# The values of stick-breaking attention: two blocks of tokens side by side in each unit of weights

## The chip, the cores and the metric

The kernel runs on one core of one Trainium2 chip. The metric is the device time of one execution in microseconds, the median of several runs. The core's engines work from instruction queues of their own and meet by semaphores: TensorE (PE in the profile; PEld is its loading of stationary operands), VectorE (DVE), ScalarE (ACT), GpSimd (POOL) and SyncE (SP), which here issues most of the transfers.

## What is computed

A decoder trunk of two layers on 512 tokens of 1024 features: a convolution layer, then an attention layer, each between two half-step SwiGLU networks. The residual stream behind the first layer is normed once and projected to keys and values that the attention layer shares. What the change touches is the attention with its projections:

```python
kv = rms_norm(h, kv_norm) @ w_kv              # 1024 -> 2 x 1024
k_flat, v_flat = jnp.split(kv, 2, axis=-1)
k_shared, v_shared = split_heads(k_flat), split_heads(v_flat)   # 16 heads of 64
...
q = split_heads(u @ attn_w_q[i])
z = einsum('bhqd,bhkd->bhqk', qb, kb) * scale
log_one_minus = where(causal, log_sigmoid(-z), 0)
log_remain = cumsum(log_one_minus, reverse) - log_one_minus
weights = where(causal, exp(log_sigmoid(z) + log_remain), 0)
out = einsum('bhqk,bhkd->bhqd', weights, vb)
```

All is in fp32, and the result must be that of fp32 products.

## The kernel before

Each fp32 operand is split into a high and a low part (`split`: a cast on ACT at L247, a subtraction on DVE at L248), and a product is three matmuls, high by high, high by low and low by high, one after the other into the same PSUM bank (`mm3`, L392 to L395; the trace shows them by these lines). Weights come as units of 128 rows by 1024 columns. `fetch` loads one on SP into `raw`, ACT casts it into `whi`, DVE makes `wlo`; each of the three has 3 buffers. `unit` hands out the next one that was begun and begins another.

Attention runs on 16 heads, two to a pair p. `project_values(i)` makes the values of four heads, i from 0 to 3: 256 columns for 512 tokens, from two units of weights, each of which holds four of the eight input chunks of 128 features. Its tokens go in four blocks b of 128. For a block, a chunk of the split input (`kvh`, `kvl`, 128 features by 128 tokens) is the stationary operand and 256 columns of the weights move; 8 chunks by 3 matmuls make 24 matmuls into one bank `pv`. Then for each of two pairs of heads, q = 0 and 1, ACT copies 128 columns into the tile `vs` (L1129, the high part) and DVE subtracts that from the bank (L1130, the low part). `project_keys(p)` makes the keys and queries of a pair of heads in banks `pk` and `pq`, each with 24 matmuls of 512 columns. `head(p, e)` is one head: scores into `z` (4 banks), a cumulative sum as matmuls of `sh` and `sl` with triangular constants into `z` (L1188), weights `w` split into `wh` and `wl` on DVE or GpSimd (L1232, L1233), products with `vs` into `av` (2 banks, L1239 and L1241), and at the end `low` on ACT (L1245) and a matmul that swaps halves (L1246). The names carry numbers: `z8_1` belongs to head 8, `pv1_0` to the values unit 1, block 0; `vs2` and `vs3` hold the values of unit 1, `vs6` and `vs7` those of unit 3.

PSUM has 8 banks; in attention 4 are of kind z, 2 of kind av, and 2 of kind pj. The banks of kind pj serve `pv`, `pk` and `pq` in turn, and at the end `po`, the output projection. Which projection is written behind which head stands in a table: unit 0 of the values and pair 0 ahead of all heads, units 1 to 3 behind heads 3, 7 and 11.

```python
PROJECTIONS = (
    (("v", 0), ("kq", 0)), (("kq", 1), ("kq", 2)), (("v", 1),), (("kq", 3), ("kq", 4)), (("v", 2),),
    (("kq", 5), ("kq", 6)), (("v", 3),), (("kq", 7),),
)
```

The order on the engines is not the written one. A scheduler places every instruction of the attention by a simulated timeline, and the matmuls of the projections fill the places in which a head waits for the other engines. So a new order in `project_values` gives new places to instructions of the heads too. The instructions on each engine run in the order that the scheduler fixed, each behind its semaphores.

Of the kernel before, what the change touches and what calls it, by code (L numbers as in the profile page):

```python
# [6 lines left out]
F32 = mybir.dt.float32  # L7
# [7 lines left out]
P = 128  # L15
D = 1024
T = 512
NC = D // P
# [67 lines left out]
PJ_BANKS = 2  # L86
# [110 lines left out]
def decoder_kernel(ctx, tc, xin, gu, dna, dnb, pw1, pw2, kq, wv, wo, out):  # L197
    nc = tc.nc
    V, A, G, PE = nc.vector, nc.scalar, nc.gpsimd, nc.tensor

    def pool(c, name, bufs=1, space=None):
        kw = {"space": space} if space is not None else {}
        return c.enter_context(tc.tile_pool(name=name, bufs=bufs, reuse_waits="tile", **kw))
# [181 lines left out]
    def unit(ahead=True):  # L385

        w = ready.pop(0)
        if ahead:
            fetch()
        return w  # L390

    def mm3(ps, w, x, first, last):  # L392
        PE.matmul(ps, w[0], x[0], start=first, stop=False)  # L393
        PE.matmul(ps, w[0], x[1], start=False, stop=False)  # L394
        PE.matmul(ps, w[1], x[0], start=False, stop=last)  # L395

    def at(pair, a, n):
        return pair[0][:, a : a + n], pair[1][:, a : a + n]
# [241 lines left out]
    with ExitStack() as c:  # L640
        wm = pool(c, "wm")
        ps = pool(c, "pswm", space=PSUM)
# [17 lines left out]
    for c in range(NC):  # L660
        n_f1.chunk(c, squares=False)
        if c in (0, 3):
            for src, raw, hi, lo in first:
                sl = slice(0, T) if c == 0 else slice(T, UNIT)
# [37 lines left out]
    with ExitStack() as c:  # L702
        cv = pool(c, "cv")
        ps = pool(c, "pscv", space=PSUM)
# [330 lines left out]
        for d in SECOND[3:]:  # L1035
            w = None if d in HELD else unit()
            pp = ps.tile([P, T], F32, name=f"pp{d}_1", tag="bank", bufs=8)[:, : T // 2]
            sl = TOKENS[1]
# [12 lines left out]
    with ExitStack() as c1:  # L1051
        kvp = pool(c1, "kvp")
        kvx = []
# [28 lines left out]
        with ExitStack() as c:  # L1082
            ap = pool(c, "at")
            ps = pool(c, "psat", space=PSUM)
# [28 lines left out]
            keys, values = {}, {}  # L1113

            def project_values(i):
                w = [unit() for h in range(2)]
                for p in (2 * i, 2 * i + 1):

                    values[p] = ap.tile([P, 4, 4, HD], F32R, name=f"vs{p}", tag="vs", bufs=4)
                for b in range(4):  # L1120
                    pv = ps.tile([P, T], F32, name=f"pv{i}_{b}", tag="pj", bufs=PJ_BANKS)
                    for k in range(NC):
                        x = at(kvx[k], b * P, P)
                        m = at(w[k // 4], (k % 4) * 256, 256)
                        mm3(pv[:, :256], x, m, k == 0, k == NC - 1)
                    for q in range(2):
                        vs = values[2 * i + q]
                        sl = pv[:, q * P : (q + 1) * P].rearrange("p (e d) -> p e d", e=2)
                        A.copy(vs[:, b, 0::3, :], sl)  # L1129
                        V.tensor_sub(vs[:, b, 1:3, :], sl, vs[:, b, 0::3, :].bitcast(F32))  # L1130

            def project_keys(p):
                w = unit()
# [134 lines left out]
            for d in range(NC):  # L1268
                w = unit()
# [200 lines left out]
```

## Time and profile before

| | |
|---|---|
| median of 3 runs | 1911.27 us (1910.86 to 1911.64) |
| the profiled execution | 1911.01 us |
| span of its trace | 1909.3 us, so 1.7 us lie outside |
| mean granted clock of TensorE in it | 0.996 |
| attention, from the first matmul of the values to the last of `po` | 1258.8 to 1541.5 us of the span |

The page of the profile gives busy time by engine and the chain of work that ended last. The windows give busy time of each engine in a stretch, the clock that TensorE was granted (1.00 is full speed) and the traffic. The waits say for which instruction of another engine a TensorE instruction stood still, with the sum, the count and the longest. The timeline gives single instructions by start and duration. A matmul is pipelined: the next may start before the duration that is shown for it is over, so the price of a matmul in a row is the step from one start to the next.

### The profile page before, as it was taken

The page shows a single profiled execution, that of the slowest core. Times are in us where ns is not written, and L with a number is a line of the kernel's source. Part 1 is how long each engine was busy: PE and PEld are TensorE (multiplying, and loading weights), DVE is VectorE, ACT ScalarE, POOL GpSimd, SP SyncE. Part 2 cuts the span into 40 slices and gives each one's busy share as a digit, 9 for nine tenths or more (in the row PEclk, how much of TensorE's full clock was granted, in tenths as well). Part 3 has the DMA queues.
Part 4 walks back from the last instruction along what each step waited for, and adds up shares of the span by engine and source line. Part 5 has one row for each costly group of instructions (what it writes and reads, how often), then busy time and mean ns, then how long its engine had stood idle before and what let it go on. Part 6 is the DMA issues. An engine that isn't in the chain of part 4 may idle for free.

```text
span 1909.3 us, 26551 instructions
## 1 busy us (share of the span) xinstructions
PE 1885.5 (99%) x10234; PEld 1631.0 (85%) x10236; DVE 1318.3 (69%) x2131; ACT 871.6 (46%) x1381; POOL 287.0 (15%) x267
## 2 busy tenths in 40 slices
PE   9999999999999999999999999999999899999997
PEld 7888888878998899898888988888888688898896
DVE  6544534589869477576765857768989668676575
ACT  5424424686644234244333423547778634243333
POOL 0211302079700000000000000004554100000001
PEclk9999999999999999999999999999999999999998
DMA  5756746444422323333433232442223133323322
GB/s 202 254 177 234 273 150 216 155 173 148 151 78 89 111 94 106 99 103 97 134 109 104 96 106 88 142 152 71 85 81 97 56 98 102 100 90 99 111 86 70
DMA packets 73678, 237.84 MB, mean 125 GB/s; under 512 B 8400, under 2 KB 10576, under 8 KB 73552
## 3 DMA queue, kind: packets, MB, share of 16 engines
q1 hardware_dynamic: 65200, 209.41, 33.8%
q10 hardware_dynamic: 8352, 26.74, 3.7%
q8 instruction: 80, 1.31, 0.3%
q14 instruction: 46, 0.38, 0.1%
HBM read 200.46 MB, written 31.46 MB: 121 GB/s over the span
## 4 chain that ended last, share of the span: by engine, by line
PE 93%; DVE 2%; ACT 2%; POOL 1%; issue 1%; DMA 0%; POOLq 0%; DVEq 0%; ACTq 0%
PE pg L393 10%; PE pg L395 10%; PE pg L394 10%; PE pd L393 8%; PE pd L394 8%; PE pd L395 8%; PE pg L553 6%; PE pg L552 6%; PE pg L551 6%; PE z L1188 1%; PE pa L393 1%; PE pa L395 1%; PE pa L394 1%; PE po L393 1%; PE po L394 1%
## 5 line engine op out<-in xcount | busy, mean ns | idle before, releaser
L247 ACT CAST whi<-raw 128x1024 fp32r<-128x1024 f32 (+2 forms) x306 | 312.3, 1023 | 646.7 <-PE pd L394 227.0
L248 DVE TENSOR_TENSOR wlo<-raw,whi 128x1024 fp32r<-128x1024 f32 (+2 forms) x306 | 369.0, 1210 | 42.8 <-ACT whi L247 42.2
L395 PE MATMUL pg<-xhi_f,wlo 128*128 128x512 f32 x896 | 349.2, 390 | 0.6 <-DVE wlo L248 0.5
L393 PE MATMUL pg<-xhi_f,whi 128*128 128x512 f32 x896 | 348.3, 390 | 1.1 <-ACT whi L247 1.1
L394 PE MATMUL pg<-xlo_f,whi 128*128 128x512 f32 x896 | 349.1, 390 | 0.0
L394 PE MATMUL pd<-hlo,whi 128*128 128x512 f32 x686 | 266.2, 389 | 0.0
L395 PE MATMUL pd<-hhi,wlo 128*128 128x512 f32 x686 | 265.1, 389 | 0.0
L393 PE MATMUL pd<-hhi,whi 128*128 128x512 f32 x686 | 264.1, 389 | 0.0
L395 PEld LDWEIGHTS pg<-xhi_f,wlo 128*128 128x128 f32 x896 | 168.3, 188 | 35.7 <-DVE wlo L248 1.4
L393 PEld LDWEIGHTS pg<-xhi_f,whi 128*128 128x128 f32 x896 | 168.4, 188 | 35.3 <-ACT whi L247 2.0
L394 PEld LDWEIGHTS pg<-xlo_f,whi 128*128 128x128 f32 x896 | 168.4, 188 | 33.6
L627 DVE SCALAR_TENSOR_TENSOR xpar<-pd,xpar 128x512 f32<-128x512 f32 x93 | 63.7, 689 | 170.1 <-PE pd L395 170.1
L395 PEld LDWEIGHTS pd<-hhi,wlo 128*128 128x128 f32 x686 | 128.8, 188 | 26.8
L394 PEld LDWEIGHTS pd<-hlo,whi 128*128 128x128 f32 x686 | 128.8, 188 | 26.8
L393 PEld LDWEIGHTS pd<-hhi,whi 128*128 128x128 f32 x686 | 128.8, 188 | 26.5
L1088 POOL TENSOR_SCALAR_AFFINE_SELECT tri<-ones 128x128 f32<-128x128 f32 x1 | 0.6, 590 | 703.7 <-DVE tu L608 703.7
L871 POOL TENSOR_TENSOR ws<-ws,pr 128x256 f32<-128x256 f32 (+1 forms) x90 | 91.0, 1023 | 58.2 <-ACT pr L869 54.6
L248 POOL TENSOR_TENSOR plo<-praw,phi 128x1024 fp32r<-128x1024 f32 x24 | 58.0, 2419 | 276.3 <-ACT phi L247 270.4
L247 ACT CAST hhi<-tu 128x512 fp32r<-128x512 f32 x88 | 54.4, 621 | 88.1 <-DVE tu L582 49.0
L882 DVE SCALAR_TENSOR_TENSOR pc<-gl,xpar,pc 128x512 f32<-128x512 f32 (+1 forms) x145 | 88.3, 646 | 4.0 <-PE pc L861 2.2
L607 DVE TENSOR_TENSOR tu<-pg,r_f 128x512 f32<-128x512 f32 x56 | 38.6, 689 | 73.9 <-PE pg L395 73.9
L552 PE MATMUL pg<-tlo,whi 128*128 128x256 f32 x256 | 72.4, 283 | 0.0
(359 smaller groups left out, 4194.1 us busy)
## 6 DMA issues: line engine op xcount, KB each, us to landing
raw<-in_gu_dram SPq DMA_DIRECT2D x174, 512.0 KB, 3.5
raw<-in_dna_dram SPq DMA_DIRECT2D x64, 512.0 KB, 3.7
praw<-in_pw_dram SPq DMA_DIRECT2D x24, 512.0 KB, 4.2
aparth<-phi ACTq DMA_DIRECT2D x24, 512.0 KB, 2.7
apartl<-plo ACTq DMA_DIRECT2D x24, 512.0 KB, 3.8
raw<-in_dnb_dram SPq DMA_DIRECT2D x32, 384.0 KB, 3.3
whi<-aparth SPq DMA_DIRECT2D x21, 512.0 KB, 3.3
wlo<-apartl SPq DMA_DIRECT2D x21, 512.0 KB, 4.2
```

The lines of the kernel that those rows point to most:

```text
L247: ins = A.copy(dst_hi, src)
L248: (G if on_pool else V).tensor_sub(dst_lo, src, dst_hi.bitcast(F32))
L393: PE.matmul(ps, w[0], x[0], start=first, stop=False)
L394: PE.matmul(ps, w[0], x[1], start=False, stop=False)
L395: PE.matmul(ps, w[1], x[0], start=False, stop=last)
L551: PE.matmul(d, a[0], b[0], start=first and q == 0, stop=False, skip_group_check=True)
L552: PE.matmul(d, a[0], b[1], start=False, stop=False, skip_group_check=True)
L553: PE.matmul(d, a[1], b[0], start=False, stop=last_, skip_group_check=True)
L607: V.tensor_mul(tu, pt[1], rb)
L627: V.scalar_tensor_tensor(res[d], pd, 0.5, res[d], op0=ALU.mult, op1=ALU.add)
L871: add("G", 1.28 * f + 0.1 * half, lambda pr=pr: G.tensor_add(accp, accp, pr()[:, at0]), r=[pr], w=[at_], rank=rank)
L882: add("V", 0.66 * f + 0.06 * half, lambda x=x, q=q: V.scalar_tensor_tensor(pc(), x(), q, pc(), op0=ALU.mult, op1=ALU.add), r=[gl], w=[pc], ...
```

## The change

`project_values` takes its blocks in pairs, (0, 1) and then (2, 3). For a pair both banks `pv` are taken at once. The four chunks of the first unit are multiplied for the first block and then for the second, then the four chunks of the second unit for the first block and for the second. Only then both blocks are copied out, in the same four steps each as before. No instruction is added or taken away; the number of matmuls, copies, subtractions and transfers is the same on every engine. Lines of the changed kernel from L1137 on are those of before plus 6.

```diff
-                for b in range(4):
-                    pv = ps.tile([P, T], F32, name=f"pv{i}_{b}", tag="pj", bufs=PJ_BANKS)
-                    for k in range(NC):
-                        x = at(kvx[k], b * P, P)
-                        m = at(w[k // 4], (k % 4) * 256, 256)
-                        mm3(pv[:, :256], x, m, k == 0, k == NC - 1)
-                    for q in range(2):
-                        vs = values[2 * i + q]
-                        sl = pv[:, q * P : (q + 1) * P].rearrange("p (e d) -> p e d", e=2)
-                        A.copy(vs[:, b, 0::3, :], sl)
-                        V.tensor_sub(vs[:, b, 1:3, :], sl, vs[:, b, 0::3, :].bitcast(F32))
+
+                for pair in ((0, 1), (2, 3)):
+                    pvs = [
+                        ps.tile([P, T], F32, name=f"pv{i}_{b}", tag="pj", bufs=PJ_BANKS)
+                        for b in pair
+                    ]
+                    for u in range(2):
+                        for b, pv in zip(pair, pvs):
+                            for k in range(4 * u, 4 * u + 4):
+                                mm3(pv[:, :256], at(kvx[k], b * P, P), at(w[u], (k % 4) * 256, 256),
+                                    k == 0, k == NC - 1)
+                    for b, pv in zip(pair, pvs):
+                        for q in range(2):
+                            vs = values[2 * i + q]
+                            sl = pv[:, q * P : (q + 1) * P].rearrange("p (e d) -> p e d", e=2)
+                            A.copy(vs[:, b, 0::3, :], sl)
+                            V.tensor_sub(vs[:, b, 1:3, :], sl, vs[:, b, 0::3, :].bitcast(F32))
```

On TensorE in unit 0, the end of the first four chunks of block 0 and what follows it. `whi204` and `wlo204` are the first unit of weights, `whi205` and `wlo205` the second; the numbers behind the names are the program's. Before:

```order
L393 MATMUL pv0_0_11495<-whi204_11307,kvh3_11115 128x256
L394 MATMUL pv0_0_11495<-wlo204_11308,kvh3_11115 128x256
L395 MATMUL pv0_0_11495<-whi204_11307,kvl3_11116 128x256
L393 MATMUL pv0_0_11495<-whi205_11340,kvh4_11121 128x256
L394 MATMUL pv0_0_11495<-wlo205_11341,kvh4_11121 128x256
L395 MATMUL pv0_0_11495<-whi205_11340,kvl4_11122 128x256
```

Now:

```order
L393 MATMUL pv0_0_11495<-whi204_11307,kvh3_11115 128x256
L394 MATMUL pv0_0_11495<-wlo204_11308,kvh3_11115 128x256
L395 MATMUL pv0_0_11495<-whi204_11307,kvl3_11116 128x256
L393 MATMUL pv0_1_11496<-whi204_11307,kvh0_11097 128x256
L394 MATMUL pv0_1_11496<-wlo204_11308,kvh0_11097 128x256
L395 MATMUL pv0_1_11496<-whi204_11307,kvl0_11098 128x256
```

The second unit of weights is needed for the first time 24 matmuls behind the first one instead of 12, and the last matmul of block 0 moves from the 24th place to the 36th. Blocks 2 and 3 of unit 0 still run one after the other on TensorE, 24 matmuls and 24, as the scheduler placed them.

On TensorE in unit 1, from the products of head 1's weights (`wh1_0`, `wl1_0`) with the values on. Before, from the last product with `wh1_0` to the first with `wl1_0`:

```order
L1239 MATMUL av1_11800<-wh1_0_11819,vs0_11493 128x256
L393 MATMUL pv1_2_12298<-whi212_11917,kvh0_11097 128x256
L394 MATMUL pv1_2_12298<-wlo212_11918,kvh0_11097 128x256
L395 MATMUL pv1_2_12298<-whi212_11917,kvl0_11098 128x256
L393 MATMUL pv1_2_12298<-whi212_11917,kvh1_11103 128x256
L394 MATMUL pv1_2_12298<-wlo212_11918,kvh1_11103 128x256
L395 MATMUL pv1_2_12298<-whi212_11917,kvl1_11104 128x256
L393 MATMUL pv1_2_12298<-whi212_11917,kvh2_11109 128x256
L394 MATMUL pv1_2_12298<-wlo212_11918,kvh2_11109 128x256
L395 MATMUL pv1_2_12298<-whi212_11917,kvl2_11110 128x256
L393 MATMUL pv1_2_12298<-whi212_11917,kvh3_11115 128x256
L1241 MATMUL av1_11800<-wl1_0_11820,vs0_11493 128x256
```

Now, from the last product with each to the first matmul of block 2:

```order
L1245 MATMUL av1_11800<-wh1_0_11819,vs0_11493 128x256
L1247 MATMUL av1_11800<-wl1_0_11820,vs0_11493 128x256
L1194 MATMUL z1_2_11796<-sh1_1_11832,none_11423 128x384
L1183 MATMUL z2_2_12056<-qs1_0_11949,ks1_0_11907 128x512
L1185 MATMUL z2_2_12056<-ql1_0_11951,ks1_0_11907 128x512
L1189 LDWEIGHTS identb_11427
L1189 MATMUL z2_2_12056<-mask_11429,identb_11427 128x128
L1194 MATMUL z1_2_11796<-sl1_1_11833,none_11423 128x384
L393 MATMUL pv1_2_12298<-whi212_11917,kvh0_11097 128x256
```

Ten matmuls of block 2 (`pv1_2`) that stood between `wh1_0` and `wl1_0` now stand behind both, and behind the sums of `sh1_1` and `sl1_1` for head 1's next group of tokens.

On DVE at the same place, before:

```order
L1130 TENSOR_TENSOR vs2_12238<-pv1_0_12240,vs2_12238 128x128
L1203 TENSOR_TENSOR sl1_2_11857<-a1_2_11851,sh1_2_11856 128x512
L1232 CAST wh1_0_11819<-w1_0_11817 128x512
L1130 TENSOR_TENSOR vs3_12239<-pv1_0_12240,vs3_12239 128x128
L1233 TENSOR_TENSOR wl1_0_11820<-w1_0_11817,wh1_0_11819 128x512
L1225 CAST sh1_1_11832<-a1_1_11827 128x384
L1130 TENSOR_TENSOR vs2_12238<-pv1_1_12269,vs2_12238 128x128
```

Now:

```order
L1209 TENSOR_TENSOR sl1_2_11857<-a1_2_11851,sh1_2_11856 128x512
L1238 CAST wh1_0_11819<-w1_0_11817 128x512
L1239 TENSOR_TENSOR wl1_0_11820<-w1_0_11817,wh1_0_11819 128x512
L1136 TENSOR_TENSOR vs2_12238<-pv1_0_12240,vs2_12238 128x128
L1231 CAST sh1_1_11832<-a1_1_11827 128x384
L1205 SCALAR_TENSOR_TENSOR a2_0_12061<-z2_0_12046,a2_0_12061 128x512
L1136 TENSOR_TENSOR vs2_12238<-pv1_1_12241,vs2_12238 128x128
L1136 TENSOR_TENSOR vs3_12239<-pv1_0_12240,vs3_12239 128x128
```

`wl1_0` follows `wh1_0` at once now, and the two subtractions that empty the bank of block 0 (`vs2` and `vs3` from `pv1_0`) stand behind it, with three steps between them, among them one for block 1.

On DVE in unit 3, where the bank of block 0 is emptied, before:

```order
L1130 TENSOR_TENSOR vs6_13558<-pv3_0_13560,vs6_13558 128x128
L1203 TENSOR_TENSOR sl10_0_13387<-a10_0_13381,sh10_0_13386 128x512
L1232 CAST wh9_2_13186<-w9_2_13184 128x512
L1199 SCALAR_TENSOR_TENSOR a10_1_13407<-z10_1_13372,a10_1_13407 128x384
L1233 TENSOR_TENSOR wl9_2_13187<-w9_2_13184,wh9_2_13186 128x512
L1130 TENSOR_TENSOR vs7_13559<-pv3_0_13560,vs7_13559 128x128
```

Now:

```order
L1209 TENSOR_TENSOR sl10_0_13387<-a10_0_13381,sh10_0_13386 128x512
L1205 SCALAR_TENSOR_TENSOR a10_2_13431<-z10_2_13376,a10_2_13431 128x512
L1208 CAST sh10_1_13412<-a10_1_13407 128x384
L1136 TENSOR_TENSOR vs6_13558<-pv3_0_13560,vs6_13558 128x128
L1208 CAST sh10_2_13436<-a10_2_13431 128x512
L1136 TENSOR_TENSOR vs7_13559<-pv3_0_13560,vs7_13559 128x128
```

The two subtractions had four steps of the heads between them, and now have one.

## Rows read from the trace of the kernel before

**Rows 1.** The page: busy time by engine; shares of the chain by engine.

```profile
PE 1885.5 (99%) x10234; PEld 1631.0 (85%) x10236; DVE 1318.3 (69%) x2131; ACT 871.6 (46%) x1381; POOL 287.0 (15%) x267
...
PE 93%; DVE 2%; ACT 2%; POOL 1%; issue 1%; DMA 0%; POOLq 0%; DVEq 0%; ACTq 0%
```

**Rows 2.** Windows: attention, its busy middle, its end; columns in the first line.

```profile
core 0: us, PE busy (x) PEld busy (x) DVE busy (x) ACT busy (x) POOL busy (x), PEclk, DMA share, GB/s
1258.80:1541.50 282.70, 275.98 (x1504) 232.05 (x1507) 234.09 (x398) 185.99 (x345) 98.10 (x92) 0.99 0.28 84
1290.00:1480.00 190.00, 188.50 (x1066) 159.50 (x1066) 175.07 (x286) 141.15 (x269) 92.54 (x87) 1.00 0.29 84
1503.00:1510.00 7.00, 5.58 (x12) 3.67 (x13) 3.20 (x5) 4.35 (x8) 0.00 (x0) 0.51 0.14 37
```

**Rows 3.** Waits of PE from 1290 to 1480: total us, times, longest.

```profile
PE z L1188 <- POOL sl L1226: 0.6, 1, 0.6
PE pq L393 <- DVE vs L1130: 0.3, 1, 0.3
PE av L1241 <- POOL wl L1233: 0.2, 1, 0.2
PE z L1188 <- POOL sl L1203: 0.2, 1, 0.2
```

**Rows 4.** Waits of PE from 1480 to 1512, the two longest sums.

```profile
PE av L1246 <- ACT low L1245: 2.5, 3, 1.2
PE po L393 <- ACT oh L247: 1.3, 1, 1.3
```

**Rows 5.** Timeline, unit 0: second unit's weights; first and 13th matmul.

```profile
1253.69 1.06 ACT L247 CAST whi<-raw 128x1024 fp32r<-128x1024 f32 x1 [1.88 <-PE pd L394]
...
1254.78 1.23 DVE L248 TENSOR_TENSOR wlo<-raw,whi 128x1024 fp32r<-128x1024 f32 x1 [0.17 <-ACT whi L247]
...
1258.83 0.36 PE L393 MATMUL pv<-whi,kvh 128*128 128x256 f32 x1 [0.88 <-ACT whi L247]
...
1260.34 0.28 PE L393 MATMUL pv<-whi,kvh 128*128 128x256 f32 x1
```

**Rows 6.** Timeline, unit 0: block 0's last matmul and subtraction; block 2's first matmul.

```profile
1261.66 0.28 PE L395 MATMUL pv<-whi,kvl 128*128 128x256 f32 x1
...
1262.91 0.29 DVE L1130 TENSOR_TENSOR vs<-pv,vs 128x128 fp32r<-128x128 f32 x1 [0.33 <-ACT vs L1129]
...
1265.47 0.36 PE L393 MATMUL pv<-whi,kvh 128*128 128x256 f32 x1
```

**Rows 7.** Timeline, units 1 and 3: block 0's last matmul and last subtraction.

```profile
1315.36 0.28 PE L395 MATMUL pv<-whi,kvl 128*128 128x256 f32 x1
...
1320.98 0.28 DVE L1130 TENSOR_TENSOR vs<-pv,vs 128x128 fp32r<-128x128 f32 x1
...
1431.86 0.28 PE L395 MATMUL pv<-whi,kvl 128*128 128x256 f32 x1
...
1436.81 0.28 DVE L1130 TENSOR_TENSOR vs<-pv,vs 128x128 fp32r<-128x128 f32 x1
```

**Rows 8.** Timeline, unit 1, at head 1's weights, in order of time.

```profile
1320.10 0.96 DVE L1232 CAST wh<-w 128x512 fp32r<-128x512 f32 x1
...
1321.11 0.39 PE L1239 MATMUL av<-wh,vs 128*128 128x256 f32 x1
...
1321.18 0.68 DVE L1233 TENSOR_TENSOR wl<-w,wh 128x512 fp32r<-128x512 f32 x1
...
1321.78 0.34 DVE L1225 CAST sh<-a 128x384 fp32r<-128x384 f32 x1
...
1322.27 1.02 POOL L1226 TENSOR_TENSOR sl<-a,sh 128x384 fp32r<-128x384 f32 x1 [1.50 <-DVE sh L1225]
```

**Rows 9.** Head 8's last product; the last matmuls of po, for spacing.

```profile
1426.04 0.39 PE L1241 MATMUL av<-wl,vs 128*128 128x512 f32 x1
...
1540.76 0.39 PE L395 MATMUL po<-oh,wlo 128*128 128x512 f32 x1
...
1541.44 0.39 PE L395 MATMUL po<-oh,wlo 128*128 128x512 f32 x1
```

**Rows 10.** Window ahead of head 8's end, columns as in rows 2.

```profile
1380.00:1426.00 46.00, 45.65 (x242) 37.47 (x241) 41.05 (x69) 32.15 (x61) 25.77 (x25) 1.00 0.25 74
```

## The prediction, made before the changed kernel was run

> **What bounds the kernel now.** The page comes first. TensorE is busy for 99% of the span and makes 93% of the chain that ended last [rows 1]. A change that keeps the number of matmuls can therefore move the time only through instants in which TensorE stands still, or through its clock. The windows show where such instants are left in attention [rows 2]. The whole of it has 282.70 - 275.98 = 6.7 us without a matmul. Its middle, 1290 to 1480, has 190.00 - 188.50 = 1.5 us at clock 1.00, and this is where values units 1 to 3 lie. The waits name them: 0.6, 0.3, 0.2 and 0.2 us, 1.3 in all [rows 3]. The other 5.2 us lie mostly at the end, where the heads run out of projections to hide behind: 2.5 us for `low` and 1.3 for `oh` [rows 4], and there are 7 us at a clock of 0.51, which is the lower of the two levels, 1.2 GHz, behind these waits [rows 2].
>
> So there is little to win, and the question is what is lost. DVE is the engine to look at: in the middle it is busy 175.07 of 190 us [rows 2], and it stands behind most of what TensorE needs from the heads.
>
> A threshold for later: 0.2% of the time is 3.8 us, about what a measurement of this kernel can tell from no change. Faster means below 1907.4, slower above 1915.1.
>
> **Part 1: the second unit of weights is wanted later (unit 0).** Before, the 13th matmul is the first to read it, 1.51 us behind the first one [rows 5], so a matmul of 256 columns costs 0.126 us. Now the 25th is, 1.5 us later. That would buy something if the second unit were late. It isn't: its low part is done at 1254.78 + 1.23 = 1256.01, and its first reader started at 1260.34, 4.3 us behind it [rows 5]. The gain is 0. In units 1 to 3 no row of TensorE waiting for `whi` or `wlo` stands among the waits [rows 3], so it is 0 there too. The first unit's last reader moves 12 matmuls ahead (1.5 us), which lets ACT begin the next cast earlier; the cast that could use it serves a wait that doesn't exist, so this is 0 as well. SP's transfers keep their place, and no queue of SP's or GpSimd's is crossed by a moved transfer.
>
> **Part 2: a bank is held longer, and emptied together with its neighbour (unit 0).** Before, block 0's bank is empty 1.54 us behind the start of its last matmul (1261.66 to 1262.91 + 0.29 [rows 6]). Now its last matmul is the 36th, 12 steps later, about 1263.1; the bank is empty at about 1264.7. Block 2, which needs it, begins at 1265.47 [rows 6]. The cover is 0.8 us, and what hides the emptying is block 1's last 12 matmuls. The cost is 0. If the cover were gone, because the second block's copies go between the first block's, it would be four more steps of some 0.3 us, 1.2 us less 0.8, so 0.4.
>
> **Part 3: places of the heads' instructions (units 1 to 3).** The copies and subtractions cost the same as before; what moves is their neighbours. In unit 1 TensorE had ten matmuls of block 2, 1.2 us, between the product with `wh1_0` and that with `wl1_0`. The order now has none there. From the rows: `wh1_0` starts at 1320.10 on DVE, and with no subtraction between them `wl1_0` starts at 1320.98 and ends at about 1321.66. TensorE would want it at 1321.23, one step behind 1321.11 [rows 8]: a wait of 0.4, with the hand-over 0.5. Then the sums: `sl1_1` on GpSimd ends at 1322.27 + 1.02 = 1323.29 [rows 8]; the start of its input `sh1_1` stays about where it was, as `wl1_0` and one subtraction have only changed places ahead of it. TensorE now has three products (0.4 us), the sum of `sh1_1` and two and a quarter matmuls of 512 columns (0.7 us with it) before it wants `sl1_1`, and comes to it at about 1322.8: a second wait of 0.5. Behind TensorE's queue at this wait stand the 24 matmuls of block 2, which are free to run but for the order, and nobody else is held by it. Together 1.0; one wait of 0.2 for `sl` that TensorE has at the same place [rows 3] goes when it comes later. Unit 1: +0.8.
>
> Units 2 and 3 have the same shape, and I did not follow each row. Above, each is bounded by unit 1's 1.0, below by nothing. In unit 2 the longest wait, 0.6 for `sl` [rows 3], lies at the same sort of place and is counted as replaced: +0.4. In unit 3 the two subtractions of block 0 stand closer together than before, so I take the middle, +0.5. Sum: 0 + 0.8 + 0.4 + 0.5 = +1.7 us. With both ends: 0 + 0.8 + 0 + 0 = +0.8 and 0.4 + 1.0 x 3 = +3.4; below nothing, all four waits of the middle go, -1.3.
>
> **Part 4: the end.** The order of the last three heads and of `po` is almost that of before. Nothing is moved there, and the 2.5, the 1.3 and the stretch at clock 0.51 stay.
>
> **The rivals.** *Nothing happens* (1911.3). The scheduler's fills may be equal in worth, since TensorE's order is a list of work that must all be done: each matmul taken out of a gap closes another. For it: only 1.5 us stand free in 190. Against it: the two places of unit 1 above. That the change doesn't do what it says is a part of this case: blocks 2 and 3 of unit 0 do run one after the other in the new order, so half of unit 0 is as before.
>
> *A, DVE sets the pace of the heads, slower.* The new order has head 8's last product behind 315 projection matmuls of 512 columns instead of 335, so it wants that head's weights 20 x 0.227 = 4.5 us sooner than 1426.04 (three steps of `po` take 1541.44 - 1540.76 = 0.68, so 0.227 each [rows 9]). If DVE can't deliver sooner, TensorE waits for 4.5 us in all, most of it ahead of 1426: 1911.3 + 4.5 = 1915.8. For it: in the 46 us ahead of that point DVE is busy for nine tenths, and TensorE has only 0.35 us free [rows 10], so neither has much in hand. Against it: DVE idles for 46.00 - 41.05 = 4.95 us ahead of that point [rows 10], and a subtraction of weights (1.23 us [rows 5]) moves behind it. It decides once the waits ahead of head 8's end pass 3.8 us.
>
> *B, the pair holds both banks, slower.* A bank of unit 1 took from 1315.36 to 1321.26, 5.9 us, to be emptied, one of unit 3 from 1431.86 to 1437.09, 5.2 [rows 7]. The order now puts work of 9728, 8576 and 6016 columns between block 0's last matmul and block 2's first, which at 0.227 per 512 is 4.3, 3.8 and 2.7 us. If the emptying stays as slow, TensorE waits 1.6, 1.8 (between 1.4 and 2.1) and 2.5: +5.9, so 1917.2. Against it: in unit 3 the new order has one step between the two subtractions instead of four. The Trainium skill, "Perfetto Trace Analysis", section "Matmuls", says that independent groups of matmuls should rotate through the PSUM banks, so that one group is emptied while the next is multiplied; two groups that end together in the only two banks speak against that. The trace agrees for unit 0 that emptying hides behind one block (1.5 us of the 3.0 that a block takes), and by the rule the cost here would be that of B.
>
> *C, the end gets better, faster.* If the heads, less tied to projections, reach the end with one matmul block more in hand, the waits of the middle go (1.3), one wait for `low` (1.2, the longest [rows 4]) and part of the stretch at 1.2 GHz. The latter has 5.58 us of work [rows 2], which at full clock is half; with what lies idle anyway I take 2.0. Together -4.5: 1906.8. Against it: the end's order is nearly unchanged, so it would have to come by timing alone.
>
> **How the numbers follow.** The sum is made against the profiled execution, 1911.01 us: 1909.3 of span and 1.7 around it. It is 0.26 under the median, so the forecast is 1912.7 on its scale and 1911.27 + 1.7 = 1913.0 on that of the median. Chances: forecast 0.40, nothing 0.16, A 0.18, B 0.08, C 0.18. The forecast with nothing gives the same side, 0.56; A and B slower, 0.26; C faster, 0.18. The range leaves out C alone, 0.18: it goes up to B, 1917.2, with 0.2 for the spread of runs, and down to 1909.0, which is the time if the gain of 2.0 at the low clock came alone, or the -1.3 with the spread. The likeliest case's own range is 1910.0 to 1914.7.
>
> **What would show it.** Unit 0: matmuls of the values keep a step of 0.126, and block 2 begins at about 1265.5; a wait there for the subtraction of `vs` would break part 2. Unit 1: a new wait of TensorE of about 0.5 at the product with `wl1_0` and another at the sum of `sl1_1`. The middle's waits, 1.3 before, become about 3. Head 8's last product comes at about 1422 to 1424; at 1426 it is A. Waits of `pv` or `pk` for a subtraction of `vs`, 1 us and more, are B. The end: a stretch of about 7 us at 0.51 as before; if it is shorter, C. What makes the sum wrong most easily is units 2 and 3, whose terms are bounds and not places.

## The result and the profile after

The changed kernel takes 1912.92 us in the median of 22 runs (1911.65 to 1914.71), the kernel before 1910.82 in the median of 22 beside them (1909.65 to 1912.13). The ratio is 1.0013, with a 95% interval from 1.0007 to 1.0019: 1.3 to 3.6 us slower, under the 3.8 us that the prediction took for the smallest difference a measurement tells. With so many runs it is told apart from nothing all the same. The forecast was 1913.0, and +1.7 against a base of 1911.27; against the base beside it the measured difference is +2.1.

The page after, first the busy time by engine and then the shares of the chain, to be held against [rows 1]:

```profile
PE 1886.5 (99%) x10234; PEld 1630.5 (85%) x10236; DVE 1320.1 (69%) x2131; ACT 872.9 (46%) x1381; POOL 281.9 (15%) x267
...
PE 92%; DVE 3%; ACT 2%; POOL 2%; issue 1%; DMA 0%; POOLq 0%; DVEq 0%; ACTq 0%
```

The counts are the same. In the chain, whose shares are rounded, TensorE has one hundredth less, and DVE and GpSimd have one more each. Where, the windows tell (columns as in [rows 2]; the middle of attention, and the stretch behind its last waits):

```profile
1290.00:1480.00 190.00, 185.87 (x1049) 156.51 (x1049) 175.67 (x284) 139.81 (x266) 87.54 (x87) 1.00 0.28 84
1507.50:1511.50 4.00, 4.00 (x10) 2.49 (x11) 2.69 (x4) 2.52 (x3) 0.00 (x0) 0.57 0.23 66
```

In the middle TensorE now has 4.1 us without a matmul, where it had 1.5 [rows 2]. The stretch at the lower clock, half of full speed, is about 3.4 us long (4 us at a mean of 0.57), where it was about 6.9 (7 us at 0.51 [rows 2]). The waits of TensorE, first from 1290 to 1480 and then the largest from 1480 on:

```profile
PE av L1247 <- DVE wl L1239: 0.9, 3, 0.4
PE av L1247 <- POOL wl L1239: 0.8, 1, 0.8
PE z L1194 <- POOL sl L1209: 0.8, 2, 0.6
PE z L1183 <- ACT w L1235: 0.8, 1, 0.8
PE z L1194 <- DVE sh L1208: 0.4, 1, 0.4
...
PE av L1252 <- ACT low L1251: 1.9, 3, 0.7
```

In the middle they add up to 3.7 us against 1.3 [rows 3], and not one of them is a wait for a subtraction of `vs`. At the end `low` costs 1.9 against 2.5 [rows 4]. By these rows the middle loses some 2.5 us, and part of it comes back at the end.

The timeline at unit 0 (first matmul, first of block 2), at unit 1, at head 8's last product and at the last matmul of `po`:

```profile
1258.20 0.36 PE L393 MATMUL pv<-whi,kvh 128*128 128x256 f32 x1 [0.88 <-ACT whi L247]
...
1264.84 0.36 PE L393 MATMUL pv<-whi,kvh 128*128 128x256 f32 x1
...
1320.47 0.38 PE L1245 MATMUL av<-wh,vs 128*128 128x256 f32 x1
1321.26 0.38 PE L1247 MATMUL av<-wl,vs 128*128 128x256 f32 x1 [0.41 <-DVE wl L1239]
...
1322.88 0.44 PE L1194 MATMUL z<-sl,none 128*128 128x384 f32 x1
...
1333.85 0.39 PE L1247 MATMUL av<-wl,vs 128*128 128x256 f32 x1 [0.34 <-DVE wl L1239]
...
1335.24 0.50 PE L1183 MATMUL z<-qs,ks 128*128 128x512 f32 x1 [0.77 <-ACT w L1235]
...
1336.70 0.27 DVE L1136 TENSOR_TENSOR vs<-pv,vs 128x128 fp32r<-128x128 f32 x1
...
1337.33 0.40 PE L393 MATMUL pk<-kvh,whi 128*128 128x512 f32 x1
...
1422.51 0.39 PE L1247 MATMUL av<-wl,vs 128*128 128x512 f32 x1
...
1543.23 0.39 PE L395 MATMUL po<-oh,wlo 128*128 128x512 f32 x1
```

In unit 0 block 2 begins 6.64 us behind the first matmul, as before (1258.83 and 1265.47 in [rows 5, 6]). In unit 1 the wait for `wl1_0` is there. Its row says 0.41, but the price is the step: 0.79 us from 1320.47 to 1321.26, where a matmul of 256 columns costs 0.12 to 0.13, so that 0.67 us are lost. A row of waits leaves part of the loss out. Attention as a whole takes 285.0 us here, from 1258.20 to 1543.23, and 282.6 before [rows 5, 9], which is 2.4 more. The whole traces differ by 1.8, because this one reached attention 0.6 us sooner, ahead of anything that the change moves.

The two waits at 1333.85 and 1335.24 have nothing between them and the end of the values but heads: the last matmul of `pv1_3` starts at 1332.04, and the next keys, `pk3`, start at 1337.33, 0.36 us behind the end of one of the subtractions that empty the values' banks (1336.70 + 0.27). In the kernel before they stood in that place:

```profile
1331.53 0.40 PE L393 MATMUL pk<-kvh,whi 128*128 128x512 f32 x1
```

### The profile page after: what moved, and what is told of

Same layout as the page of the kernel before. It is cut to its first block, busy times and chain, and to the rows that moved or that the text cites. A ratio compares the mean times of both kernels' runs of the same rounds, so it can differ in the third digit from the quotient of the medians.

```text
span 1911.1 us, 26552 instructions
## 1 busy us (share of the span) xinstructions
PE 1886.5 (99%) x10234; PEld 1630.5 (85%) x10236; DVE 1320.1 (69%) x2131; ACT 872.9 (46%) x1381; POOL 281.9 (15%) x267
## 4 chain that ended last, share of the span: by engine, by line
PE 92%; DVE 3%; ACT 2%; POOL 2%; issue 1%; DMA 0%; POOLq 0%; DVEq 0%; ACTq 0%
PE pg L395 10%; PE pg L393 10%; PE pg L394 10%; PE pd L394 8%; PE pd L393 8%; PE pd L395 8%; PE pg L553 6%; PE pg L552 6%; PE pg L551 6%; PE z L1194 1%; PE pa L393 1%; PE pa L394 1%; PE pa L395 1%; POOL ws L871 1%; PE po L394 1%
```

## The experiments

Each of the twelve kernels ran beside the kernel before on one chip. At the outset stood the theory of the prediction, later called N, and its rivals A and B. N says that the cost comes from the new neighbours on DVE and from where the heads' instructions stand. After the first four runs B was widened into a second theory, H: a pair holds both banks of kind pj until it is emptied, so no other projection can be placed beside the heads in that time, whether the lack shows as a wait for `vs` or as bare waits of the heads (waits with no projection to fill them).

**One unit at a time.** Each of the four takes the pairs in one values unit and leaves the loop over single blocks in the others:

```diff
-                for b in range(4):
+                if i == 1:              # 0, 1, 2 or 3
+                    for pair in ((0, 1), (2, 3)):
+                        ...
+                else:
+                    for b in range(4):
+                        ...
```

> Only values unit 0 works in pairs; units 1 to 3 are as before. The order of DVE, ACT and GpSimd is then that of before, and on TensorE 24 matmuls of unit 0 stand elsewhere. Theory (the cost lies in where the heads' instructions stand in units 1 to 3): 0, within 0.4 us of the kernel before, and the third block of unit 0 starts 6.6 us behind the first matmul as before. If the pair's hold on the banks costs at unit 0 too: a wait of TensorE of up to 0.4 us at the third block. If the later need of the second unit of weights were a gain: up to -1.5 us.

Measured: 1911.67 us against 1910.86, ratio 1.0003 (0.9994 to 1.0011). That is no difference, and there is no new wait at unit 0; a gain of 1.5 is excluded by the interval (it reaches to -1.1). The profiled run shows one wait of 0.7 for `wl` in unit 3's stretch that the kernel before, with the same order of DVE, lacks. A single trace may differ by that much from the next.

> Only unit 1 works in pairs. Theory: most of the whole change's +2.1 us is here. The changed kernel's trace has new waits of 0.4, 0.3 and 0.8 us in the 16 us behind unit 1, against 0.6 and 0.25 us further back in the kernel before: +1.0 to +1.9. If the vector engine paces all heads (rival A): unit 1 alone brings fewer than 20 matmuls ahead of head 8's end, so less than +0.7. If the banks are held too long (rival B): +1.6 as a wait of the third block's first matmul for a subtraction of vs.

Measured: 1911.56 us, ratio 1.0005 (0.9996 to 1.0014), so +0.7, between -0.8 and +2.7. The new waits are where they were in the changed kernel, but their cost doesn't last. The windows of this run, 1290 to 1340 and 1340 to 1390:

```profile
1290.00:1340.00 50.00, 48.03 (x279) 40.54 (x279) 44.69 (x73) 35.10 (x69) 21.79 (x23) 1.00 0.29 85
1340.00:1390.00 50.00, 50.00 (x292) 43.02 (x291) 44.76 (x77) 35.80 (x69) 25.74 (x26) 1.00 0.23 64
```

TensorE is busy for 48.03 and 50.00 us in them, and in the kernel before for 49.74 and 49.39. So 1.7 us are lost behind unit 1, and 0.6 are won back 50 us later, where the wait of 0.6 for `sl` [rows 3] isn't met: TensorE comes later and finds the result there. The expected cost was the sum of the waits, +1.0 to +1.9. The median lies below that, but the interval covers it all, so the run doesn't decide against it.

> Only unit 2 works in pairs. Theory: the waits of the changed kernel behind unit 2 (0.64 us) take the place of those before (0.61 and 0.25 us): -0.4 to +0.4. Rival B: +1.8, at the third block's first matmul. Rival A: up to +4.5, since unit 2 is the one ahead of head 8.

Measured: 1914.52 us, ratio 1.0017 (1.0008 to 1.0026), +3.7 by the medians, where the whole change has +2.1. It is rival B's wait for a bank, though at the next keys and not, as B had it, at the third block. The waits of TensorE from 1370 to 1410 in this run:

```profile
PE pk L393 <- DVE vs L1136: 2.0, 1, 2.0
PE av L1259 <- POOL wl L1251: 0.8, 1, 0.8
PE z L1206 <- POOL sl L1244: 0.6, 1, 0.6
PE av L1259 <- DVE wl L1251: 0.5, 1, 0.5
```

And its timeline: the last matmul of the values, the last of the heads ahead of the keys, the subtraction that frees a bank, the keys that need it, and the first and the last of the slow steps behind them; at the end the window over these:

```profile
1388.76 0.28 PE L395 MATMUL pv<-whi,kvl 128*128 128x256 f32 x1
...
1393.24 0.49 PE L1259 MATMUL av<-wl,vs 128*128 128x512 f32 x1 [0.53 <-DVE wl L1251]
...
1395.45 0.28 DVE L1136 TENSOR_TENSOR vs<-pv,vs 128x128 fp32r<-128x128 f32 x1
...
1395.78 0.50 PE L393 MATMUL pk<-kvh,whi 128*128 128x512 f32 x1 [2.04 <-DVE vs L1136]
...
1396.58 0.61 PE L393 MATMUL pk<-kvh,whi 128*128 128x512 f32 x1
...
1399.98 0.41 PE L395 MATMUL pk<-kvh,wlo 128*128 128x512 f32 x1
...
1396.00:1400.00 4.00, 4.00 (x12) 3.10 (x12) 3.46 (x6) 1.57 (x3) 2.18 (x2) 0.57 0.36 124
```

For 7 us behind the last value TensorE has only heads to work on, and waits for `wl` twice; then the keys wait 2.0 us for the bank. Behind that the clock is at its lower level, 1.2 GHz: eight steps from 1396.58 to 1399.98, 3.40 us, where eight steps of 0.227 [rows 9] are 1.82. That is 1.6 us more, which stand in no row of waits. The 2.0 and the 1.6 together make 3.6, close to the +3.7, but that is not the whole account. The place also has the two waits for `wl`, 1.3 by the rows, and by the step the wait for the bank is longer too: 2.54 us from 1393.24 to 1395.78, where 512 columns cost 0.23. The profiled execution took 1913.74, only 2.9 above the median of the kernel before, so other places must have given something back. The expectation of the theory, -0.4 to +0.4, falls. That of B was 1.8, and lacked the clock. A allowed up to 4.5, but 335 projection matmuls stand ahead of head 8's last product in this trace, as in the kernel before, so what A rests on doesn't happen here.

> Only unit 3 works in pairs. Theory: the changed kernel has new waits of 0.4 and 0.85 us behind unit 3 and lacks 0.3 there and 1.0 at the end of attention: -0.3 to +1.0. Rival B: +2.5, at the third block's first matmul. Rival A: 0, since head 8 ends ahead of unit 3.

Measured: 1912.79 us, ratio 1.0011 (1.0002 to 1.002), +1.9. The median lies above what the theory allowed (+1.0 at most) and A (0), but the interval, 0.4 to 3.8 us, reaches into the theory's range. No wait for a bank is in it. Its middle is as busy as before (188.33 of 190 us), and its longest new waits lie behind 1480, in the last heads (`wl` 1.0, `sh` 0.8). Its cause isn't settled by a further run.

The three units come to 0.7 + 3.7 + 1.9 = 6.3 us by the medians, and all four together to 2.1. The costs of the places don't add. The likely reason, not shown, is that what the scheduler does at one unit changes what it finds at the next.

**The bank taken out of the way.** A block of values fills 256 of the 512 columns of a bank. So a pair can share one bank and leave the other free, with the same instructions in number:

```diff
-                    pvs = [
-                        ps.tile([P, T], F32, name=f"pv{i}_{b}", tag="pj", bufs=PJ_BANKS)
-                        for b in pair
-                    ]
+                    both = ps.tile([P, T], F32, name=f"pv{i}_{pair[0]}", tag="pj", bufs=PJ_BANKS)
+                    pvs = [both[:, :256], both[:, 256:]]
...
+                            s, e = j == 0 and k == 0, j == 1 and k == NC - 1
+                            PE.matmul(pvs[j], x[0], m[0], start=s, stop=False, skip_group_check=True)
```

Only the first matmul of a pair has its start flag set. The Trainium skill, "PSUM — Partial Sum Buffer", section "The four PSUM rules", says why: a start clears, for the whole bank, the marks by which a later matmul adds to what is there, so a second start would make the other block's next matmul overwrite its sum. No run here shows the other way.

> The change with one edit: both blocks of a pair share one bank, 256 columns each, so a pair holds one of the two banks of kind pj and not both. Theory H (a pair that holds both banks leaves the scheduler no projection matmuls to put into the heads' waits until it is emptied): the cost goes, -1.0 to +0.7 us against the kernel before, and no waits above 0.5 us stand within 20 us behind unit 1. Theory N (the cost comes from the new neighbours on DVE, whatever the banks): +1.5 to +3, with waits for wl and w behind unit 1 as in the changed kernel.

> Control for the run above: two blocks share one bank, but run one after the other, each over all eight chunks, as before the change. H: within 1 us of the kernel before and of the run above. N: like the kernel before, and 1.5 to 3 below the run above.

Measured: 1915.18 us with pairs, ratio 1.0021 (1.0012 to 1.0029), and 1914.74 for the control without them, 1.0022 (1.0012 to 1.0032). By the medians H had the difference of the two right, 0.4 us, and N, which wanted 1.5 to 3 between them, didn't; the two intervals lie over each other and are too wide to exclude the lower part of N's range. H had the level wrong: both are some 4 us above the kernel before. The first waits of the one with pairs show where:

```profile
PE z L1203 <- POOL sl L1218: 1.5, 1, 1.5
PE av L1256 <- DVE wl L1248: 1.1, 1, 1.1
PE av L1256 <- POOL wl L1248: 0.9, 1, 0.9
```

All three lie between 1450 and 1458, behind the values of unit 3, and the control has its longest close by, at 1459.6:

```profile
PE av L1252 <- DVE wh L1245: 2.3, 2, 1.9
```

From 1290 up to 1450 one wait is left in the run with pairs, 0.8 for `sl` at unit 2. The sharing does away with the trouble behind unit 1 and makes one behind unit 3, with or without pairs. What is missing there is again a projection. The last matmul of the keys in the run with pairs, a subtraction on DVE, and the first matmul of the queries (`pq`):

```profile
1449.93 0.39 PE L395 MATMUL pk<-kvh,wlo 128*128 128x512 f32 x1
...
1457.41 0.27 DVE L1138 TENSOR_TENSOR vs<-pv,vs 128x128 fp32r<-128x128 f32 x1
...
1459.27 0.78 PE L393 MATMUL pq<-xhi_mix,whi 128*128 128x512 f32 x1
```

The banks go in turn, so `pq` takes the one of unit 3's second pair, and a shared bank is empty only when both of its blocks are out, after four subtractions instead of two. The one shown is the last of them, and it ends at 1457.68. For 9 us the heads run bare. The control has the same gap, from 1454.88 to 1464.03, with the last subtraction done at 1463.58; the kernel before has 1.8 us between its `pk` and `pq`. So the 4 us seem to be the same lack of a bank in another shape; this is read from the traces, and no run tests it by itself.

The other way to a free bank is a third one for projections, taken from the four of z:

```diff
-Z_BANKS = 4
+Z_BANKS = 3
...
-PJ_BANKS = 2
+PJ_BANKS = 3
```

> The kernel before with a third bank for projections, taken from the four of z. Both theories: a few us off, with waits at z for its bank; it is the base for the next run.

> The changed kernel with the same third bank. H: no slower than the run above by more than 0.7 us, since the third block or the next keys find a bank. N: 1.5 to 3 us above the run above.

Measured: 1921.43 us without pairs and 1921.59 with them, ratios 1.0058 (1.0045 to 1.0071) and 1.0057 (1.0045 to 1.007). The exchange of a bank of z for one of pj costs 10.5 us, and on that base the pairs cost 0.2. By the medians this again is H's difference and not N's, but the intervals are wide (5 us each) and the kernel is far from the one in question.

**The bank, unit by unit.** The sharing of one bank in a single unit, or in two, with units left as before elsewhere, tells the place apart from the rest:

> Unit 1 alone in pairs, as in the run with unit 1 alone, but with both blocks of a pair in one bank. H: TensorE has no wait of 0.3 us or more from 1315 to 1340 us of the span (there were three, 0.4, 0.3 and 0.8 us, with two banks), since the third block and the next keys stand there. N: the same waits stay. The whole time is not settled by either, since the places behind change too: 1909.5 to 1913.

Measured: 1910.49 us, ratio 0.9996 (0.9988 to 1.0005). TensorE has no wait at all between 1315 and 1340. The next keys start at

```profile
1330.32 0.40 PE L393 MATMUL pk<-kvh,whi 128*128 128x512 f32 x1
```

instead of 1337.33, and fill the place in which `wl` and `w` were waited for. By the time alone this isn't told apart from unit 1 with two banks (+0.7); by the waits it is. Unit 3, in single blocks here, has a wait of 1.4 for a bank (`pq` for a subtraction of `vs`), where the kernel before has 0.3 [rows 3]: a full pool isn't the pairs' alone.

> Unit 2 alone in pairs, both blocks of a pair in one bank. H: the wait of 2.0 us of the next keys for a subtraction of vs, which unit 2 alone had with two banks, is gone, and the time falls by 1.5 to 3 us against that run, to 1911.5 to 1913. N: the wait or one like it stays, and the time is within 1 us of that run (1914.5).

Measured: 1909.17 us, ratio 0.9991 (0.9982 to 1.0), against 1914.52 for the same unit in pairs with two banks, whose interval (1.0008 to 1.0026) lies wholly above. The waits from 1370 to 1410, and the change from the last of the values to the keys:

```profile
PE z L1215 <- POOL sl L1253: 0.6, 1, 0.6
PE av L1266 <- DVE wh L1259: 0.3, 1, 0.3
...
1389.87 0.36 PE L1131 MATMUL pv<-whi,kvl 128*128 128x256 f32 x1
1390.07 0.39 PE L393 MATMUL pk<-kvh,whi 128*128 128x512 f32 x1
```

The keys follow the last matmul of the values by 0.2 us instead of 7.0, though the subtractions behind that come no earlier (1395.28 for the next one on DVE, 1394.79 with two banks). The wait of 2.0 and the low clock are gone. The same pairs, the same number of subtractions, and 5.4 us between them by the medians: for unit 2 this shows H. (H's own figure, 1911.5 to 1913, was too high. The two profiled executions, 1910.49 here and 1913.74 there, are 3.3 apart.)

> Units 1 and 2 in pairs with one bank a pair, units 0 and 3 as before the change. In the run with all units so, TensorE's idle time up to unit 3 was 1.9 us below that of the kernel before, and 6.8 above it at unit 3. H: without unit 3 the gain stays, 1909 to 1911. N: no gain, 1911 to 1915.

Measured: 1908.97 us, ratio 0.9991 (0.9982 to 1.0). This is the best of all, 1.9 us below the kernel before by the medians, at the very edge of what the interval grants, and 4 below the changed kernel. Its middle isn't better than that of before, though:

```profile
1290.00:1480.00 190.00, 187.62 (x1068) 159.53 (x1066) 176.13 (x285) 140.34 (x269) 86.15 (x86) 1.00 0.28 84
```

TensorE is idle there for 2.4 us against 1.5 [rows 2]. The gain lies behind it, from 1480 to 1512, first in this run and then in the kernel before:

```profile
1480.00:1512.00 32.00, 28.19 (x131) 21.07 (x132) 25.16 (x43) 21.90 (x42) 6.80 (x6) 0.95 0.15 46
```

```profile
1480.00:1512.00 32.00, 26.82 (x126) 20.26 (x125) 23.81 (x39) 22.16 (x41) 5.56 (x5) 0.89 0.09 25
```

TensorE has 1.4 us more of work in it and a higher clock. The time came out as expected, and not from the place. Unit 3 works in single blocks here, and `pq` finds its bank 0.2 us behind the last subtraction (1451.43 + 0.28), where the heads had 9 us without a projection in the run that shares the bank in every unit:

```profile
1451.43 0.28 DVE L1157 TENSOR_TENSOR vs<-pv,vs 128x128 fp32r<-128x128 f32 x1
...
1451.92 0.39 PE L393 MATMUL pq<-xhi_mix,whi 128*128 128x512 f32 x1
```

> Control for units 1 and 2 in pairs with one bank a pair (1908.97): the same sharing of a bank, but block after block over all eight chunks, so without the interleaving over the units of weights. If the bank alone decides (H): within 1.5 us of that run, 1908 to 1910.5. If the interleaving itself brings the gain once the bank is out of the way: 1910.5 to 1913.

Measured: 1911.64 us, ratio 1.0005 (0.9996 to 1.0014), 2.7 above the run with pairs by the medians. H's figure is missed, and the time lies in the range of the other expectation, a gain from the interleaving itself. But the intervals of the two overlap between 0.9996 and 1.0, and the windows of this run, the middle and the end, put the difference elsewhere:

```profile
1290.00:1480.00 190.00, 188.52 (x1068) 159.71 (x1069) 178.45 (x286) 142.44 (x269) 89.95 (x87) 1.00 0.29 84
1480.00:1512.00 32.00, 26.81 (x119) 19.25 (x118) 22.88 (x38) 21.53 (x41) 5.69 (x5) 0.90 0.08 22
```

In the middle, where units 1 and 2 lie, this run idles less than the one with pairs (188.52 busy against 187.62). It falls behind from 1480 on, where its TensorE has 26.81 us of work against 28.19 and the lower clock, as in the kernel before. So a gain of the interleaving at its own place isn't seen, and over all four units the two writings came out alike.

## Why the prediction was right, and where it was not

**The whole.** The time and the side came as forecast, with the mechanism named: waits of the heads in units 1 to 3, and nothing from the weights. The sum is better than its terms, though: the middle loses more than the +1.7 that was forecast for it (2.4 more by the rows of waits alone), and the end, said to stay, gives some back. That +1.7 came so near to +2.1 is in good part luck.

**Part 1** held. The second unit's weights were ready in time before, and wanting them 1.5 us later changed nothing: unit 0 alone gave +0.8, with zero in its interval, and block 2 of unit 0 begins 6.64 us behind the first matmul in both kernels.

**Part 2** held for unit 0: no wait at block 2.

**Part 3** is right in kind and wrong in each size. In unit 1 the wait for `wl1_0` was put at 0.5 and is 0.41 by its row. The second one, 0.5 for `sl1_1`, isn't there: TensorE reaches that sum at 1322.88 and doesn't stand still. The wait of 0.2 for `sl` that was to go is still there: it lies ahead of the place (at 1319.68 before, at 1319.03 after), so coming later to the place could not remove it. What the term left out are the two waits of 0.34 and 0.77 twelve to fourteen us further on, behind the second pair of blocks, where the order shown wasn't followed. The step that failed is "behind TensorE's queue at this wait stand the 24 matmuls of block 2, which are free to run but for the order": they are free, but the work behind them, the next keys, isn't, since both banks are full. Units 2 and 3 were bounded by 0 and 1.0 each and cost 3.7 and 1.9 by the medians when alone. In the whole change they don't. By the rows of waits unit 2 lost 0.2 less than before (0.64 for `sl`, at 1383.44, against 0.6 and 0.25), where +0.4 was forecast. Unit 3 lost 1.2 more (0.43 for `sh` at 1440.50, 0.19 and 0.85 for `wl` at 1451.88 and 1466.39, against 0.3), where it was +0.5, and unit 1 lost 1.5 more, where it was +0.8. The terms come near in their sum alone, and the bound of 1.0 was no bound.

**Part 4** fell. The end was said to stay. It gained: 1.9 against 2.5 for `low`, and 3.4 us at the lower clock against 6.9.

**Rival A** fell: head 8's last product starts at 1422.51, and not at 1426. With 315 projection matmuls ahead of it instead of 335 it comes 3.5 us sooner, so DVE did deliver.

**Rival B** was given 0.08, and has the cause as far as the runs show one. It was priced as a wait of `pv` for `vs`, and there is none in the changed kernel. The lack shows in another way: the scheduler queued no keys while the bank was full and let the heads go bare, and the waits are for `wl` and `w`; `pk3` starts 0.36 us behind one of the subtractions that empty the banks. In unit 2 alone the wait for the bank itself came, 2.0 us for the 1.8 that B had, but at another matmul than B's, so that the two figures agree by chance. The rule of the Trainium skill that the prediction weighed there ("Perfetto Trace Analysis", section "Matmuls": one group is emptied while the next is multiplied, in another bank) agrees with the runs at unit 2: with both banks in one pair it costs 3.7 us, and with one bank left free it is 1.7 below the kernel before by the medians, with zero at the edge of its interval.

**Rival C**'s mechanism came in part, the 0.6 of `low` and half of the stretch at the low clock, and was outweighed.

**What stays open:** the +1.9 of unit 3 alone, why the costs of the units don't add, and whether the late `pq` is all of the 4 us that a shared bank in every unit costs. Each comes with an order of the scheduler that differs from the next in hundreds of places, and no run here holds the rest of the order still. Nor is it shown that H is the whole of the changed kernel's +2.1. Shown are its waits at unit 1, 1.5 of the 2.4 us by which the rows of the middle grew, which go when the bank is free, though the time alone doesn't tell those two runs apart. Shown too is the wait for the bank in unit 2, which doesn't occur in the changed kernel. Its waits behind unit 3 no run explains.

## What to carry to other kernels

Before two accumulations are run side by side, count the banks they hold against what else wants one: what fills the waits of the neighbouring work may be the third user of that pool. A full pool need not show as a wait for the bank; look for stretches in which the filler is missing, and for its start right behind the instruction that empties a bank. Two sums in one bank spare a bank while they are formed, but hold it until both are out. And where a scheduler sets the order, price a change by stretches and expect the parts not to add.

## What the runs showed of the hardware

A wait of 2.0 us of TensorE in unit 2 alone, which was itself preceded by waits of 0.8 and 0.5, was followed by 3.4 us at 1.2 GHz, though TensorE worked without a pause in them: 1.6 us that no row of waits holds. The waits of up to 0.8 in the middle of the changed kernel left the clock at 1.00. Behind unit 3 of the pairs in one bank the clock fell again, with waits of 0.9, 1.1 and 1.5 that ended at 1451.43, 1454.93 and 1457.19. In the first of these two windows of that run it is still at full speed, in the second at 0.55:

```profile
1452.00:1456.00 4.00, 2.25 (x11) 1.32 (x9) 4.00 (x7) 2.90 (x6) 2.48 (x4) 1.00 0.51 175
1456.00:1460.00 4.00, 2.81 (x9) 2.31 (x10) 3.94 (x9) 3.02 (x7) 3.00 (x3) 0.55 0.52 162
```

The longest wait alone doesn't tell when it falls. In unit 1 with one bank it fell behind three waits of only 0.29, 0.36 and 0.31, which ended at 1486.67, 1487.54 and 1488.72 among the last heads:

```profile
1488.00:1492.00 4.00, 3.69 (x13) 2.87 (x14) 3.31 (x7) 3.65 (x8) 1.23 (x2) 0.62 0.01 4
```

And two sums may be open in one bank at once, in columns of their own, when only the first matmul has its start flag set: four of the twelve kernels ran that way.
